# One PSUM pool for a whole decoder kernel, the norm's matmul inside the first up product, and wider operand operations

## The chip, the cores and the metric

The kernel runs on one core of a Trainium2 chip. The metric is the device time of one execution in microseconds (us); "before" is the kernel ahead of the change, "after" the changed one. Its engines are named as in the profile: PE (TensorE, matmuls), DVE (VectorE), ACT (ScalarE), POOL (GpSimd) and SP (SyncE, which here issues the weight loads). PSUM, the memory that PE writes to, has eight banks of 512 fp32 columns for each of the 128 partitions.

## The reference

A trunk of two pre-norm layers for one sequence of 512 tokens with 16 learned meta tokens ahead of them, model width 1024. Layer 0 mixes tokens by causal pooling, layer 1 by stick-breaking attention with 16 heads of 64; behind each mixer stands a SwiGLU FFN with 2816 hidden columns, and at the end a norm. Everything is float32.

```python
def rmsnorm(x, g):
    y = x * lax.rsqrt(jnp.mean(x * x, axis=-1, keepdims=True) + EPS)
    return y * g
def swiglu(h, w_gate, w_up, w_down):
    return (jax.nn.silu(h @ w_gate) * (h @ w_up)) @ w_down
# layer 0: window means (2, 4, 8, 16) minus the input, by group of 256 columns, times w, times scale
# layer 1: z = q k^T / 8; a = exp(log_sigmoid(z) + sum over later keys of log_sigmoid(-z)), strictly causal; a v, times w_o
for each layer:  x = x + mixer(rmsnorm(x)); x = x + swiglu(rmsnorm(x))
out = rmsnorm(x) without the meta tokens
```

## The kernel before, in words

**Numbers.** Every fp32 product is three matmuls on parts: a tile is cast to a shorter form on ACT ("hi", names ending in h) and the rest is subtracted on DVE ("lo", names ending in l); `mm3` (L106) issues hi·hi, hi·lo and lo·hi. Weights come by DMA into `wraw` (six buffers, SP's queue) and are split by `wsplit`: cast on ACT (L92), subtraction on DVE (L97).

**Stages.** The activations lie transposed as eight chunks h of 128 model columns by 528 tokens.

1. Start: norm of the tokens, pooling by matmuls with band matrices (`pool`), the group products (`mix`), and the residual add into h (L266). When a chunk is complete, `Norm.chunk` makes its hi and lo parts, times the gain (L152, L153), and adds its square to a running sum `acc` (L161; the last add is L128).
2. FFN of layer 0, 528 tokens. The hidden columns are worked in 22 steps f of 128. For f = 0, 1, 2 (`plain`) the gate and up products `pp` take the unnormalised hi and lo chunks; the norm's factor is multiplied in when a product is read out of PSUM (L364). The factor is one ones-matmul over `acc` (`norm_bcast`, L173, named fb0p), a reciprocal root on ACT (L135) and a Newton step on DVE (L136 to L139, result fb0r). From f = 3 on (`strassen`) gate and up are computed together as a 2 by 2 block product with seven instead of eight half products; their token operands are seven combinations of the normalised chunks. `operands` makes these once for each FFN: it multiplies in the norm (xn, L381), forms differences (t, L387) and splits into xh (ACT, L389) and xl (DVE, L390). The seven products run in three PSUM tiles pa, pb, pc; in between ACT copies the running values out (L412). The down product `pd` goes in six rounds; the down matmuls of one round are laid between the gate and up matmuls of the next. Its sums are added to h by DVE (L304).
3. Attention: eight head pairs p. Projections `pj`, scores z, sigmoids on ACT (L576), the running product over keys as a scan on DVE (L581), the weights sg (L583), their transposes on PE (`t`, L594 and L607), the product with v (`po`, L633). Output products `pw` come in three parts, for the pairs 0 to 1, 2 to 4 and 5 to 7; each is added to h by DVE (L660). The last part builds the next norm's chunks as it goes, with the names f1uh, f1ul, f1sq.
4. FFN of layer 1, on 512 tokens (fb1p and fb1r are its norm's factor), then the final norm and the store.

**What sets the order.** The program is written as one stream. A scheduler arranges each engine's instructions by its own estimate of times, bound by data dependences, by buffers coming free, and by `tc.issue_after(x)`, which keeps what is issued inside it behind instruction x. Each engine then works in that order, one after the other. An instruction that waits holds everything behind it on its engine. PSUM comes from four pools in turn, one for each stage (`phase`: ps0 with eight one-bank buffers, ps1 with six "w" and two "d", ps2 with four "one" and two "two" of two banks, ps3 like ps1). A new pool can be written only when the old one's tiles are read.

## Time and profile before

| what | value |
|---|---|
| runs | 1235.87, 1058.43, 1060.87 us; median 1060.87 |
| profiled execution | 1062.8 us, span 1061.0 us, mean granted PE clock 0.985 |
| busy in the span | PE 1023.1 (96%), DVE 856.6 (81%), ACT 556.9 (52%), POOL 6.2 (1%) |
| PE's longest waits | 4.1 (first product of FFN 1), 3.6 (last pair's transposes), 2.2 (first product of FFN 0), 2.1 (first Strassen products of FFN 0) |

Rows of the profile name the engine, the line of the kernel, the operation, the tiles as out<-in and their sizes, the count, and in brackets how long the engine was idle before it and what released it. In the table of stretches each engine's busy time stands with its number of instructions; a granted clock of 1.00 is full speed. A PE row's duration reaches past the start of the next row, since matmuls overlap; the distance of starts is what one costs. The stretches that matter: start until 39 us, FFN 0 to 408, attention to 691, FFN 1 to 1052, the store to 1061.

### The profile page before, as it was taken

Reading aid. Unit: us, or ns where it says so; the run is one execution under the profiler, and the core shown is the slowest. Engines: PE = TensorE matmul, PEld = TensorE weight load, DVE = VectorE, ACT = ScalarE, POOL = GpSimd, SP = SyncE. Lnnn points to the kernel's source line nnn. Section 1 sums busy time; section 2 is a strip of 40 time slices with the busy share of each in tenths; the row PEclk is TensorE's granted clock in tenths of the full one; section 3 lists DMA queues with packets and bytes.
Section 4 is the critical chain, followed back from the end, with each engine's and each line's share of the span. In section 5 each row is a group of like instructions: output and inputs, shape, how many; then the busy total and the mean of one; then the engine's idle time right before and its main releaser. Section 6 shows DMA issues by size and latency. Waiting matters only on the chain.

```text
span 1061.0 us, 18586 instructions
## 1 busy us (share of the span) xinstructions
PE 1023.1 (96%) x7302; PEld 949.3 (89%) x7302; DVE 856.6 (81%) x1529; ACT 556.9 (52%) x1131; POOL 6.2 (1%) x16
## 2 busy tenths in 40 slices
PE   8998999999999999999999998989999999999997
PEld 6997999999999998998888886867899999999985
DVE  7899987888878777678888987779977877788755
ACT  7555645454444455455555454555655444455544
POOL 1000000000000010000000000000000000000000
PEclk9999999999999999999999998989999999999999
DMA  9212323333333332211111211211223223333302
GB/s 351 72 51 69 128 94 100 101 100 100 100 100 100 99 120 82 78 40 61 40 51 37 69 58 66 80 62 58 100 100 115 84 100 99 100 100 120 109 31 80
DMA packets 43112, 95.73 MB, mean 90 GB/s; under 512 B 3328, under 2 KB 20096, under 8 KB 43024
## 3 DMA queue, kind: packets, MB, share of 16 engines
q1 hardware_dynamic: 42272, 93.40, 26.2%
q8 instruction: 57, 0.93, 0.3%
q10 hardware_dynamic: 752, 1.14, 0.3%
q14 instruction: 31, 0.25, 0.1%
HBM read 92.43 MB, written 2.10 MB: 89 GB/s over the span
## 4 chain that ended last, share of the span: by engine, by line
PE 78%; DVE 17%; issue 2%; ACT 1%; DMA 1%; SPq 0%; ACTq 0%; DVEq 0%
PE pb L106 15%; PE pd L106 11%; PE pd L331 11%; PE pa L106 10%; PE pc L106 10%; PE pj L106 9%; PE pp L106 4%; DVE kp L581 2%; PE pw L106 2%; PE z L567 2%; DVE xl L390 1%; DVE a L619 1%; PE t L594 1%; DVE t L387 1%; DVE sg L583 1%
## 5 line engine op out<-in xcount | busy, mean ns | idle before, releaser
L304 DVE TENSOR_TENSOR h<-pd,h 128x264 f32<-128x264 f32 x96 | 40.9, 427 | 14.0 <-PE pd L106 14.0
L92 ACT CAST ws_3h<-rgate 128x512 fp32r<-128x512 f32 x38 | 23.6, 620 | 53.3 <-PE pb L106 47.8
L581 DVE TENSOR_TENSOR_SCAN kp<-kp,estrip 128x1344 f32<-128x1344 f32 x16 | 47.3, 2954 | 3.8 <-ACT kp L576 3.4
L92 ACT CAST ws_4h<-s 128x512 fp32r<-128x512 f32 x38 | 23.6, 621 | 46.6 <-PE pa L106 27.7
L92 ACT CAST ws_5h<-s 128x512 fp32r<-128x512 f32 x38 | 23.6, 621 | 45.8 <-PE pb L106 34.7
L433 DVE TENSOR_TENSOR u<-pb,m 128x264 f32<-128x264 f32 (+1 forms) x38 | 16.3, 428 | 38.6 <-PE pb L106 38.6
L106 PE MATMUL pa<-xl,ws_0h 128*128 128x264 f32 (+1 forms) x152 | 43.3, 285 | 3.1 <-DVE xl L390 3.0
L106 PE MATMUL pb<-xl,ws_1h 128*128 128x264 f32 (+1 forms) x152 | 43.3, 285 | 1.0 <-DVE xl L390 1.0
L106 PE MATMUL pc<-xl,ws_2h 128*128 128x264 f32 (+1 forms) x152 | 43.1, 283 | 0.9 <-DVE xl L390 0.9
L106 PE MATMUL pb<-xh,ws_1h 128*128 128x264 f32 (+1 forms) x152 | 43.6, 287 | 0.2 <-ACT xh L389 0.2
L106 PE MATMUL pa<-xh,ws_3h 128*128 128x264 f32 (+1 forms) x152 | 43.6, 287 | 0.0
L106 PE MATMUL pa<-xl,ws_3h 128*128 128x264 f32 (+1 forms) x152 | 43.5, 286 | 0.0
L106 PE MATMUL pa<-xh,ws_3l 128*128 128x264 f32 (+1 forms) x152 | 43.3, 285 | 0.0
L106 PE MATMUL pc<-xh,ws_2l 128*128 128x264 f32 (+1 forms) x152 | 43.2, 284 | 0.0
L106 PE MATMUL pa<-xh,ws_0h 128*128 128x264 f32 (+1 forms) x152 | 43.1, 284 | 0.0
L106 PE MATMUL pb<-xh,ws_6l 128*128 128x264 f32 (+1 forms) x152 | 43.0, 283 | 0.0
L106 PE MATMUL pa<-xh,ws_0l 128*128 128x264 f32 (+1 forms) x152 | 43.0, 283 | 0.0
L106 PE MATMUL pb<-xh,ws_4l 128*128 128x264 f32 (+1 forms) x152 | 43.0, 283 | 0.0
L106 PE MATMUL pc<-xl,ws_5h 128*128 128x264 f32 (+1 forms) x152 | 42.9, 283 | 0.0
L106 PE MATMUL pb<-xh,ws_1l 128*128 128x264 f32 (+1 forms) x152 | 42.9, 283 | 0.0
L106 PE MATMUL pb<-xl,ws_4h 128*128 128x264 f32 (+1 forms) x152 | 42.9, 282 | 0.0
L106 PE MATMUL pc<-xh,ws_5h 128*128 128x264 f32 (+1 forms) x152 | 42.9, 282 | 0.0
(1179 smaller groups left out, 4110.9 us busy)
## 6 DMA issues: line engine op xcount, KB each, us to landing
rgate<-in_ffn_w_gate_dram SPq DMA_DIRECT2D x44, 512.0 KB, 3.5
rup<-in_ffn_w_up_dram SPq DMA_DIRECT2D x44, 512.0 KB, 3.5
rd<-in_ffn_w_down_dram SPq DMA_DIRECT2D x42, 512.0 KB, 3.6
rq<-in_sb_w_qkv_dram SPq DMA_DIRECT2D x8, 512.0 KB, 3.5
rk<-in_sb_w_qkv_dram SPq DMA_DIRECT2D x8, 512.0 KB, 3.4
rv<-in_sb_w_qkv_dram SPq DMA_DIRECT2D x8, 512.0 KB, 3.4
rwo<-in_sb_w_o_dram SPq DMA_DIRECT2D x8, 384.0 KB, 3.0
h<-in_x_t_dram SPq DMA_DIRECT2D x8, 264.0 KB, 6.9
```

The source lines that it names most:

```text
L92: nc.scalar.copy(hi, v[:, j:j + w])
L106: last = nc.tensor.matmul(o, lhsT=w, rhs=xx[:, sl], start=start and i == 0, stop=stop and i == 2, skip_group_check=more)
L304: nc.vector.tensor_tensor(out=hv, in0=pd, in1=hv, op=ALU.add)
L331: nc.tensor.matmul(pd, lhsT=hid[j][x_][:, ts], rhs=w_[:, sl], start=r > 0 and i + j == 0, stop=j == len(hid) - 1 and i == 2, skip_group_ch ...
L387: nc.vector.tensor_tensor(out=o, in0=a, in1=b, op=ALU.subtract)
L390: nc.vector.tensor_tensor(out=xl[i][:, m, :], in0=o, in1=f32(xh[i][:, m, :]), op=ALU.subtract)
L433: tt(out=u[:, a], in0=pb, in1=m1, op=ALU.add)
L567: nc.tensor.matmul(tz[:, hd, c:c + k1 - k0], lhsT=qq[hs, i * P:(i + 1) * P], rhs=kk[hs, k0:k1], start=j == 0 and c == 0, stop=False, skip_ ...
L581: nc.vector.tensor_tensor_scan(kp[:, hd, ::-1], kp[:, hd, ::-1], estrip[:, ::-1], 1.0, op0=ALU.mult, op1=ALU.max)
L583: return nc.vector.tensor_tensor(out=sg[:, hd, 0:STRIP - 1], in0=sg[:, hd, 0:STRIP - 1], in1=kp[:, hd, 1:STRIP], op=ALU.mult).ins
L594: nc.tensor.transpose(o, sg[:, c0:c0 + n], ident)
L619: nc.vector.scalar_tensor_tensor(a0[r, i], f32(a0h[r]), lo_rows[r], p2[r, 256:384], op0=ALU.mult, op1=ALU.add)
```

## The change

1. **One PSUM pool** for the whole program, with tags two (2 buffers of two banks), c and d (2 buffers of one bank each). At the start "any" takes turns over all of it; in the attention "one" takes turns over c and d. In `strassen` pa and pb become the two halves of one two-bank tile `pab`, pc takes c. A tile is tracked as a whole: an instruction that writes one half waits for reads of the other half too.
2. **The norm's matmul** stands inside the first up product, behind its fifth chunk (`FB = 4`), instead of behind the first gate product in the program's text. The weight splits of f = 1 are issued behind the last add of `acc` (`norm.done`), those of f = 2 behind the norm's factor. Gate and up are read out of PSUM after both products; SiLU works in place.
3. **Operands two chunks at a time**: the differences t are 8 instead of 16 DVE operations, xl 14 instead of 28, xh 14 instead of 28 ACT operations, each twice as wide.
4. **The attention's PE order is fixed**: `queued` issues each step behind the last instruction of the step before.

```diff
+    psum = ctx.enter_context(tc.tile_pool(name="psum", bufs=1, space=bass.MemoryType.PSUM))
+    turn = {"one": 0, "any": 0, "pair": 0}
     def ps(name, tag, banks=1):
+        i = turn.get(tag, 0)
+        turn[tag] = i + 1
+        if tag == "any":
+            if i % 8 in (0, 1, 4, 5):
+                if i % 2 == 0:
+                    turn["tile"] = ps(name, "two", 2)
+                return turn["tile"][:, i % 2]
+            tag = "cd"[i % 2]
+        if tag == "one":
+            tag = "cd"[i % 2]
         shape = [P, 512] if banks == 1 else [P, banks, 512]
-        return psum["pool"].tile(shape, F32, tag=tag, name=name, bufs=psum["bufs"][tag])
+        return psum.tile(shape, F32, tag=tag, name=name, bufs=2)
+    def ps_pair(name):
+        i = turn["pair"]
+        turn["pair"] = i + 1
+        if i % 3 == 2:
+            return [ps(f"{name}{j}", "c") for j in range(2)]
+        pt = ps(name, "two", 2)
+        return [pt[:, 0], pt[:, 1]]
...
             def plain(f):
-                parts = [wsplit(raw_gu(kind, f), f"w{kind}{f}") for kind in ("gate", "up")]
-                g, sg, u = (gw(f"{i}{f}") for i in ("g", "sg", "u"))
-                for dst, (wh, wl) in zip((g, u), parts):
-                    pts = [ps(f"pp{f}", "w")[:, :sl.stop - sl.start] for sl in pieces]
+                parts = []
+                for kind in ("gate", "up"):
+                    with tc.issue_after(norm.done if f == 1 else fst[1]) if f else nullcontext():
+                        parts.append(wsplit(raw_gu(kind, f), f"w{kind}{f}"))
+                g, u = (gw(f"{i}{f}") for i in "gu")
+                prods = []
+                both = ps_pair(f"pp{f}") if not full else None
+                for i, (dst, (wh, wl)) in enumerate(zip((g, u), parts)):
...
                     for k in range(KC):
-                        mm3([(t, slice(t0 + sl.start, t0 + sl.stop)) for t, sl in zip(pts, pieces)], wh[k], wl[k],
-                            uh[k], ul[k], k == 0, k == KC - 1)
-                    if not fst:
-                        fst.extend((norm_bcast([acc], f"fb{layer}", "d"), last_rstd[0]))
+                        with tc.issue_after(mark) if mark else nullcontext():
+                            last = mm3(...)
+                        if i == 1 and k == FB and not fst:
+                            with tc.issue_after(last):
+                                fst.extend((norm_bcast([acc], f"fb{layer}", "d"), last_rstd[0]))
+                            mark = last_bcast[0]
...
             def operands():
-                for m in range(4):
+                for m in (0, 2):
...
                     for i, o in enumerate((b11, t2, t1, b21, t3, b22, t4)):
-                        nc.scalar.copy(xh[i][:, m, :], o)
-                        nc.vector.tensor_tensor(out=xl[i][:, m, :], in0=o, in1=f32(xh[i][:, m, :]), op=ALU.subtract)
+                        hi, lo = xh[i][:, m:m + 2, :], xl[i][:, m:m + 2, :]
+                        nc.scalar.copy(hi, o)
+                        nc.vector.tensor_tensor(out=lo, in0=o, in1=f32(hi), op=ALU.subtract)
...
-                pa, pb, pc = [ps(f"p{i}{f}", "w")[:, :n] for i in "abc"]
+                pab = ps(f"pab{f}", "two", 2)
+                pa, pb, pc = pab[:, 0, :n], pab[:, 1, :n], ps(f"pc{f}", "c")[:, :n]
...
                 prod(pa, wa11, 0, True)
-                m1 = keep(pa, "m1")
+                nc.scalar.copy(m1, pa)
                 prod(pb, ws2, 1, True)
...
+        pos = []
+        def queue():
+            return tc.issue_after(pos[0]) if pos else nullcontext()
+        def queued(*steps):
+            for st in steps:
+                with queue():
+                    pos[:] = [st()]
...
-            mark = None
-            for st in before:
-                mark = st()
-            with tc.issue_after(mark) if mark else nullcontext():
-                sc.group(0)
-                mark = sc.group(1)
-            for st in between:
-                with tc.issue_after(mark):
-                    mark = st()
-            with tc.issue_after(mark):
-                sc.group(2)
+            queued(*before, lambda: (sc.group(0), sc.group(1))[1], *between, lambda: sc.group(2))
```

How instructions move is shown at three places. On DVE at the start of the second FFN, before: f1sq is the norm's running sum, fb1t the Newton step, wgate2l the low part of f = 2's gate weights. This is the end of the sum.

```order
L161 TENSOR_TENSOR f1sq_8384<-f1sq_8384,f1sq_8521 128x528
L128 SCALAR_TENSOR_TENSOR f1sq_8384<-f1sq_8543,f1sq_8384 128x528
L97 TENSOR_TENSOR wgate2l_8849<-rgate_2_8846,wgate2h_8848 128x512
L97 TENSOR_TENSOR wgate2l_8853<-rgate_2_8846,wgate2h_8852 128x512
L136 TENSOR_TENSOR fb1t<-fb1r 128x528
L97 TENSOR_TENSOR wup2l_8859<-rup_2_8856,wup2h_8858 128x512
```

The same place on DVE in the changed kernel, where wgate1l and wup1l are f = 1's weights:

```order
L147 SCALAR_TENSOR_TENSOR f1sq_8237<-f1sq_8396,f1sq_8237 128x528
L116 TENSOR_TENSOR wgate1l_8567<-rgate_1_8564,wgate1h_8566 128x512
L116 TENSOR_TENSOR wgate1l_8571<-rgate_1_8564,wgate1h_8570 128x512
L116 TENSOR_TENSOR wup1l_8577<-rup_1_8574,wup1h_8576 128x512
L116 TENSOR_TENSOR wup1l_8581<-rup_1_8574,wup1h_8580 128x512
L155 TENSOR_TENSOR fb1t<-fb1r 128x528
L157 SCALAR_TENSOR_TENSOR fb1t<-fb1p_8479,fb1t 128x264
```

f = 1's subtractions have moved from among the sum's adds to behind it, and f = 2's from ahead of the Newton step to behind it. At the start of the first FFN the same four stand behind the sum. On PE the norm's matmul (fb0p, fb1p) stands behind 82 and 43 matmuls of the products, before behind 89 and 33.

On PE at the last head pair, before: z_416 is the last score group, pw_2 and pw_3 are output products of the pairs 2 to 4.

```order
L106 MATMUL pw_2_8163<-os4h,wo_2l_8160 128x512
L106 MATMUL pw_3_8178<-os2h,wo_3h_8174 128x512
L106 MATMUL pw_3_8178<-os2l,wo_3h_8174 128x512
L106 MATMUL pw_3_8178<-os2h,wo_3l_8175 128x512
L567 MATMUL z_416_8136<-qk_1h,qk_0h 128x400 [waits PE_49,Activation_49]
```

The same place on PE in the changed kernel:

```order
L125 MATMUL pw_1_7978<-os4l,wo_1h_7974 128x512
L125 MATMUL pw_1_7978<-os4h,wo_1l_7975 128x512
L598 MATMUL z_416_7989<-qk_1h,qk_0h 128x400 x2
L598 MATMUL z_416_7989<-qk_1h,qk_0h 128x16 x2
L598 MATMUL z_416_7989<-qk_1l,qk_0h 128x400 x2
```

The scores now follow pw_1 directly; the nine matmuls of pw_2 and the first three of pw_3 stand behind them.

On PE in a Strassen step of the first FFN, in the changed kernel: pc is the third product, pd_0 a down product, pab with ws_1h the first matmul of pb.

```order
L125 MATMUL pc_2507<-xl_547,ws_2h_2486 128x264
L125 MATMUL pc_2507<-xh_540,ws_2l_2487 128x264
L125 MATMUL pd_0_2618<-hh_1760,wd_2_0h_2614 128x264 [waits DVE_49,Activation_49]
L125 MATMUL pd_0_2618<-hl_1761,wd_2_0h_2614 128x264
L125 MATMUL pd_0_2632<-hh_1760,wd_2_0h_2614 128x264 [waits DVE_49]
L125 MATMUL pd_0_2632<-hl_1761,wd_2_0h_2614 128x264
L125 MATMUL pab_2506<-xh_539,ws_1h_2482 128x264 [waits Activation_49]
```

Before, pb's first matmul stands there without a wait, and behind other matmuls:

```order
L106 MATMUL pd_7_2547<-hh_1651,wd_1_7h_2529 128x264
L106 MATMUL pd_7_2547<-hl_1652,wd_1_7h_2529 128x264
L106 MATMUL pd_7_2547<-hh_1651,wd_1_7l_2530 128x264
L106 MATMUL pb_2602<-xh_551,ws_1h_2577 128x264
L106 MATMUL pb_2602<-xl_558,ws_1h_2577 128x264
```

Now that matmul waits for ACT's copy of the other half, which reads pa's product; between pa's last matmul and the wait stand typically sixteen matmuls.

More of the change, by code (lines that the diff above doesn't have):

```diff
@@ L126, in add_eps @@
     def add_eps(out, sq, acc):
-        nc.vector.scalar_tensor_tensor(out, sq, D * EPS / P, acc, op0=ALU.add, op1=ALU.add)
-    last_rstd = []
+        return nc.vector.scalar_tensor_tensor(out, sq, D * EPS / P, acc, op0=ALU.add, op1=ALU.add).ins
+    last_rstd, last_bcast = [], []
     def rstd_of(parts, r, t):
@@ L172, in norm_bcast @@
             for i, acc in enumerate(accs):
-                nc.tensor.matmul(p, lhsT=ones, rhs=acc[:, o:o + h], start=i == 0, stop=i == len(accs) - 1)
+                last_bcast[:] = [nc.tensor.matmul(p, lhsT=ones, rhs=acc[:, o:o + h], start=i == 0,
+                                                  stop=i == len(accs) - 1).ins]
             parts.append((p, slice(o, o + h)))
@@ L179, in trunk @@
     norm = Norm(16, "f0")
-    with tc.tile_pool(name="start", bufs=1) as sp, phase("ps0", one=8):
+    with tc.tile_pool(name="start", bufs=1) as sp:
         nc.scalar.activation(sp.tile([P, 1], F32, name="table"), ones[:, 0:1], AF.Abs_reciprocal_sqrt)
@@ L232, in trunk @@
         nc.vector.memset(warm, 0.0)
-        pw = ps("warm", "one")
+        pw = ps("warm", "any")
         for _ in range(WARM):
@@ L244, in trunk @@
                 cs = slice(c * P, (c + 1) * P)
-                pp = ps(f"pool{c}{hf}", "one")[:, :HALF]
+                pp = ps(f"pool{c}{hf}", "any")[:, :HALF]
                 for j, (i, off) in enumerate(terms):
@@ L259, in trunk @@
                 g, d = c // 2, c % 2
-                pm = ps(f"mix{c}{hf}", "one")[:, :HALF]
+                pm = ps(f"mix{c}{hf}", "any")[:, :HALF]
                 for k in range(2):
@@ L375, in operands @@
                 rb = fst[0]
[L376 removed]
+                for m in (0, 2):
                     xn = []
                     for c in (m, m + 4):
[L379 to L382 removed]
+                        t = fp.tile([P, 2, L], F32, tag="xn", name=f"xn{c}", bufs=2)
+                        for j in range(2):
+                            gc = gains[:, gcol + c + j:gcol + c + j + 1]
+                            nc.vector.scalar_tensor_tensor(t[:, j, tok], hT[c + j][:, tok], gc, rb[:, tok],
+                                                           op0=ALU.mult, op1=ALU.mult)
                         xn.append(t)
[L384 removed]
+                    b11, b12, b21, b22 = [t[:, :, s] for t in xn for s in halves]
                     t1, t2, t3, t4 = [wk(f"t{i}") for i in range(4)]
@@ L480, in before_attention @@
         return norms[0].chunk
-    with phase("ps1", w=6, d=2):
-        ffn(0, 16, norm, before_attention)
-    with tc.tile_pool(name="att", bufs=1) as ap, phase("ps2", one=4, two=2):
+    ffn(0, 16, norm, before_attention)
+    with tc.tile_pool(name="att", bufs=1) as ap:
         uh, ul, acc = norms[0].uh, norms[0].ul, norms[0].acc
@@ L599, in turned @@
             p1, p2 = ps(f"t1{p}{hd}", "two", 2), ps(f"t2{p}{hd}", "one")
-            for i in range(4):
-                tr(p1[:, 0, i * P:(i + 1) * P], i, 1)
-            for i in range(1, 4):
-                tr(p1[:, 1, (i - 1) * P:i * P], i, 2)
-            tr(p1[:, 1, 384:512], 3, 4)
-            for i in range(2, 4):
-                tr(p2[:, (i - 2) * P:(i - 1) * P], i, 3)
-            nc.tensor.transpose(p2[:, 256:384], am.rearrange("p a b -> p (a b)"), ident)
+            with queue():
+                for i in range(4):
+                    tr(p1[:, 0, i * P:(i + 1) * P], i, 1)
+                for i in range(1, 4):
+                    tr(p1[:, 1, (i - 1) * P:i * P], i, 2)
+                tr(p1[:, 1, 384:512], 3, 4)
+                for i in range(2, 4):
+                    tr(p2[:, (i - 2) * P:(i - 1) * P], i, 3)
+                pos[:] = [nc.tensor.transpose(p2[:, 256:384], am.rearrange("p a b -> p (a b)"), ident).ins]
             a1 = [ap.tile([P, 2, 512], F32R, tag="a1", name=f"a1{p}{hd}{n}", bufs=2) for n in "hl"]
@@ L686, in trunk @@
         sg = begin(0, got, [], steps[3:4])
-        steps[4]()
+        queued(steps[4])
         values()
         nxt, steps, values = proj(1)
-        for st in steps[:3]:
-            st()
+        queued(*steps[:3])
         early, w = wo(0, 2), wo(2, 5)
@@ L696, in trunk @@
             w0 = turned(p, 0, sg[:, 0])
-            for st in steps[3:] if p + 1 < NP else w[4:6]:
-                st()
+            queued(*(steps[3:] if p + 1 < NP else w[4:6]))
             if p + 1 < NP:
                 values()
-            attend(p, 0, w0, v, of)
+            queued(lambda: attend(p, 0, w0, v, of))
             w1 = turned(p, 1, sg[:, 1])
```

56 lines of the change are left out of this document (24 added, 32 removed).

## The prediction, on record before the changed kernel ran

> **What bounds the kernel now.** I read the page first, then the busy time by stretches of the run, then what TensorE (PE) waited for, and last single instructions at the places where it waited. All times are microseconds of one profiled execution, whose span is 1061.0 and whose own time is 1062.8; the median of the three runs shown, 1060.87, lies 1.9 below it. The page gives busy time, share and instruction count of each engine, and the engines' shares of the chain of waits:
>
> ```profile
> PE 1023.1 (96%) x7302; PEld 949.3 (89%) x7302; DVE 856.6 (81%) x1529; ACT 556.9 (52%) x1131; POOL 6.2 (1%) x16
> PE 78%; DVE 17%; issue 2%; ACT 1%; DMA 1%; SPq 0%; ACTq 0%; DVEq 0%
> ```
>
> PE is idle for 1061.0 − 1023.1 = 38 in all, and the change leaves every matmul product as it is. Only this idle time and the time lost at a lower clock can be won. The stretches tell where both lie (start:end and width, then busy time and instructions of PE, PEld, DVE, ACT, POOL, the granted PE clock, DMA share, GB/s):
>
> ```profile
> 26.00:40.00 14.00, 11.81 (x93) 11.63 (x93) 12.84 (x28) 7.68 (x14) 0.00 (x0) 0.96 0.26 90
> 40.00:60.00 20.00, 20.00 (x155) 19.87 (x154) 16.92 (x31) 10.92 (x20) 0.00 (x0) 0.94 0.21 70
> 80.00:90.00 10.00, 6.39 (x34) 5.51 (x33) 10.00 (x24) 4.30 (x13) 0.00 (x0) 0.83 0.15 52
> ...
> 250.00:381.00 131.00, 131.00 (x1078) 131.00 (x1077) 100.99 (x189) 64.06 (x129) 0.00 (x0) 1.00 0.32 105
> ...
> 410.00:440.00 30.00, 28.38 (x185) 24.79 (x184) 17.72 (x22) 15.04 (x26) 0.00 (x0) 0.94 0.15 53
> ...
> 500.00:670.00 170.00, 160.91 (x1096) 140.21 (x1096) 142.90 (x201) 89.73 (x192) 0.00 (x0) 0.98 0.16 51
> ...
> 690.00:710.00 20.00, 15.85 (x58) 12.47 (x57) 14.03 (x23) 9.21 (x16) 0.00 (x0) 0.83 0.23 79
> 710.00:740.00 30.00, 28.95 (x139) 23.65 (x137) 29.97 (x61) 16.65 (x35) 0.00 (x0) 1.00 0.15 53
> 740.00:760.00 20.00, 18.47 (x123) 17.03 (x124) 18.99 (x42) 13.44 (x32) 0.00 (x0) 0.91 0.23 79
> ...
> 800.00:1030.00 230.00, 230.00 (x1603) 214.41 (x1602) 179.21 (x318) 116.66 (x238) 0.00 (x0) 1.00 0.30 99
> 1030.00:1061.00 31.00, 23.06 (x120) 19.43 (x118) 16.76 (x47) 12.48 (x31) 0.00 (x0) 0.92 0.18 68
> ```
>
> In the steady parts of both FFNs (250:381, 800:1030) PE is never idle and the clock is 1.00: there is nothing to win there, only to lose. The borders are otherwise: around the start of the first FFN (26 to 90), the end of attention and the start of the second FFN (690 to 760), where DVE is full (10.00 of 10, 29.97 of 30) and PE waits for it. What PE waited for (total, times, longest):
>
> ```profile
> PE pp L106 <- DVE h L660: 4.1, 1, 4.1
> PE t L594 <- DVE sg L583: 3.6, 1, 3.6
> PE pa L106 <- DVE xl L390: 3.0, 3, 2.1
> PE pp L106 <- DVE h L266: 2.2, 1, 2.2
> ```
>
> Four places: the first product of each FFN, the last head pair of attention, and the Strassen products waiting for their low operands xl. In all of them DVE is the releaser.
>
> **The change part by part. Start of the first FFN.** From the last mix matmuls to the operands:
>
> ```profile
> 36.59 0.28 PE L106 MATMUL mix<-ph,pw1l 128*128 128x264 f32 x1
> 39.06 0.56 PE L106 MATMUL pp<-f0uh,wgate0h 128*128 128x264 f32 x1 [2.19 <-DVE h L266]
> 47.92 0.71 DVE L128 SCALAR_TENSOR_TENSOR f0sq<-f0sq,f0sq 128x528 f32<-128x528 f32 x1
> 51.42 1.05 PE L173 MATMUL fb0p<-f0sq,ones 128*128 128x264 f32 x4
> 52.93 0.71 DVE L136 TENSOR_TENSOR fb0t<-fb0r 128x528 f32<-128x528 f32 x1 [2.16 <-ACT fb0r L135]
> 97.20 1.11 DVE L390 TENSOR_TENSOR xl<-t,xh 128x264 fp32r<-128x264 f32 x3
> ```
>
> The first product waited for the last read out of the old PSUM pool. With one pool it starts behind the mixes, so the 2.19 goes. Half of it may come back ahead of it: pool and mix products that are halves of one two-bank tile wait until both halves of its last use are read. Neither decides: what is late next is the norm. Its sum is complete at 47.92 + 0.71 = 48.6, but its matmul stood behind the whole product and ran at 51.42. Now it stands inside the up product; it can run at about 48.9. The four subtractions of f=1's weights now stand between the sum and L155 (L136 before) on DVE, in order, and hold it until 48.6 + 4 × 0.6 = about 51.1 instead of 52.93, with 0.6 as one of them takes in the next rows: 1.8 gained. These are DVE's starts for a wide operation and two half as wide:
>
> ```profile
> 60.44 0.70 DVE L367 TENSOR_TENSOR u<-sg,u 128x528 f32<-128x528 f32 x1
> 61.06 0.42 DVE L387 TENSOR_TENSOR t<-xn 128x264 f32<-128x264 f32 x1
> 61.40 0.76 DVE L364 TENSOR_TENSOR g<-pp,fb0r 128x264 f32<-128x264 f32 x2
> ```
>
> From start to start, 0.62 for 528 columns and 0.34 for 264. So one wide operation for two saves 2 × 0.34 − 0.62 = 0.06, and the 8 + 14 fewer operations of the operands save 22 × 0.06 = 1.3 in each FFN. ACT's 14 fewer casts are worth nothing, since DVE, not ACT, is full here. [...]
>
> Between L155 and the last xl, DVE worked 97.20 + 1.11 − 52.93 = 45.4. By the new order it has 1.3 less for the wider operations, three weight subtractions more (3 × 0.6) and four evictions of down products fewer (4 × 0.34): 44.5. The last xl is then ready at 51.1 + 44.5 = 95.6, some 2.7 earlier. But those evictions are missing because some 40 down matmuls now lie behind the last wait instead of before it, at 0.12 each almost 5 of PE time, about half of which PE can do while the last operands arrive. I take +0.5 for this border: from −1.5 (all 40 left over) to +4 (PE finds them all in the time that it now idles).
>
> **First FFN to attention.** The first projection is now laid between the last down products. PE is idle there for 30 − 28.38 = 1.6, and the norm that the attention needs comes when it came: 0, from −1 to +1.
>
> **Attention.** The fixed order of pairs 0 to 4 is that of the scheduler before, on PE, DVE and ACT. In pairs 5 and 6 the transposes go behind all four output products instead of two. Of the 170 − 160.91 = 9.1 idle in that stretch, 3.6 is the last pair's; the rest is spread over all pairs: +0.5, from 0 to 1.5. The last pair:
>
> ```profile
> 648.84 0.40 PE L106 MATMUL pw<-os2h,wo_3h 128*128 128x512 f32 x1
> 649.07 0.39 PE L106 MATMUL pw<-os2l,wo_3h 128*128 128x512 f32 x1
> ...
> 649.63 0.46 PE L567 MATMUL z<-qk_1h,qk_0h 64*128 64x400 f32 x4
> 651.83 2.96 DVE L581 TENSOR_TENSOR_SCAN kp<-kp,estrip 128x1344 f32<-128x1344 f32 x1 [1.64 <-ACT kp L576]
> 655.76 1.55 DVE L583 TENSOR_TENSOR sg<-sg,kp 128x1343 f32<-128x1343 f32 x1
> 657.45 2.36 PE L594 MATMUL t<-consts,sg 128*128 128x128 f32 x10 [3.59 <-DVE sg L583]
> ```
>
> The last scores z stood behind twelve matmuls of pw_2 and pw_3; now they stand ahead of them: 12 × 0.23 = 2.8 earlier. The scan, the weights and the transposes follow, so the 3.59 shrinks to about 0.8: +2.8, and everything after it moves up alike, since it hangs on sg. Bounds: 0, if the output evictions on DVE (0.7 each) slip ahead of the scan and eat it; +4.5, if the clock loss behind the gap (PEclk 0.98 of 170, so 3.4) half goes too.
>
> **Attention to the second FFN.**
>
> ```profile
> 690.62 0.40 PE L106 MATMUL pw<-os7h,wo_7l 128*128 128x512 f32 x1
> 695.16 0.77 PE L106 MATMUL pp<-f1uh,wgate0h 128*128 128x512 f32 x1 [4.15 <-DVE h L660]
> 700.49 0.71 DVE L128 SCALAR_TENSOR_TENSOR f1sq<-f1sq,f1sq 128x528 f32<-128x528 f32 x1
> 705.60 0.61 PE L173 MATMUL fb1p<-f1sq,ones 128*128 128x264 f32 x2
> 708.29 0.71 DVE L136 TENSOR_TENSOR fb1t<-fb1r 128x528 f32<-128x528 f32 x1 [2.30 <-ACT fb1r L135]
> 748.38 0.75 DVE L390 TENSOR_TENSOR xl<-t,xh 128x256 fp32r<-128x256 f32 x2
> ```
>
> Here the product now starts at 690.9 and runs at 0.23 a matmul; before, it ran at half clock for 6.8 (0.17 of the clock missing over 20 is 3.4 lost). 43 matmuls then stand ahead of the norm's: 690.9 + 42 × 0.23 = 700.5, against 705.60. The sum must be there by then: it ended at 701.2, and the four subtractions that moved behind it (4 × 0.6 = 2.4) bring it to 698.8. L155 follows at the old distance (2.7), at 703.2 against 708.29: 5.1. DVE's work from there to the last xl, 749.1 − 708.29 = 40.8, loses 1.3 and gains two subtractions of f=2's weights that stood before L136: −0.1. PE reaches the same count of matmuls at about 744.8 instead of 749.9: +5. Lower bound +2, if the product's own chunks arrive late (PE takes them as fast as DVE makes them, and half the gain goes); upper +7, if the half clock at 740:760 (0.91 of 20, so 1.8 lost) goes as well.
>
> **Steady parts.** With pa and pb as halves of one tile, pb's first product waits for ACT's copy of pa. Both PE and all behind it would stand:
>
> ```profile
> L412 ACT COPY m<-pa x38: 354/372/383, 94.7 to 1020.0; 128x264 f32<-128x264 f32 x19, 128x256 f32<-128x256 f32 x19
> ```
>
> The copy takes 0.37; between the end of pa's product and that wait stand, by the new order, typically 12 pc and 4 down matmuls, 16 × 0.12 = 1.9, which cover it: 0. ACT is busy for 64.06 of 131, so it is seldom far behind. The SiLU written in place and the scratch tiles regrouped by two change no operation's size: 0. The weight loads on SP's queue wait for raw buffers that the moved subtractions free 2.4 later; DMA is busy for 0.23 of 690:710, and the loads run ahead by several tiles: 0. The tail (31 − 23.06 idle) keeps its work: 0.
>
> **Sum**: 0.5 + 0 + 0.5 + 2.8 + 5 = 8.8, so 1062.8 − 8.8 = 1054.0; against the median, 1052.1. I take 1053.
>
> **The rivals.** *All the gaps go.* The waits of the four places (4.1 + 3.6 + 3.0 + 2.2 = 12.9) and the clock lost at 26:60, 80:90, 500:670 and 690:760 (0.6 + 1.2 + 1.7 + 3.4 + 3.4 + 1.8 = 12.1): 25, hence 1038, more than 2% faster. For it: each has DVE as its releaser, and DVE is given less to do. Against: DVE stays full through both operand stages, and so PE must wait somewhere. The clock fell after the 2.19 gap at 39.06 (0.56 for a matmul instead of 0.28). [...] Chance 0.12.
>
> *No gain.* DVE stays the bound through both operand stages, and what the norm gains is lost to the work moved behind it: only the last pair's 2.8 is left and the first border loses 1.5: about 1061. For it: the first border's working above. Chance 0.25.
>
> *Slower: the shared tile.* At three places of each of the 38 Strassen steps (pb's first matmul, pa's second product, pb's third) PE waits for ACT's copy. If ACT stands behind its own casts there, each shows up. Uncovered, 114 × 0.37 = 42, so 1054 + 42 = 1096; beyond 2% it needs 1082 − 1054 = 28, which is 0.25 a wait. Against: the 1.9 of cover and ACT's 52%. For: the steady rows have no slack at all. Chance 0.07.
>
> *The change doesn't do what it says*: fixing the attention's order fixes what stood there already. That is in the sum, which counts only pairs 5 to 7.
>
> **How the numbers follow.** Forecast 0.56, no gain 0.25, all gaps go 0.12, shared tile 0.07. A measurement of this kernel tells about 2% (21) from no change: faster means under 1040, slower over 1082. The forecast's own range from its bounds is 1062.8 − 18 to 1062.8 + 0.5, so 1045 to 1063. The no-gain rival lies inside it. Reaching half-way towards the rival on the fast side, and by 2 over the upper bound for the scatter of the three runs (1058.43 against 1060.87), 1041 to 1065 should hold 8 in 10. Faster 0.12, within 2% 0.81, slower 0.07.
>
> **What would show it.** Right: pp directly behind mix and pw; fb1p about 5 earlier from the last pw; the wait of t on sg below 1.5; the rows 250:381 and 800:1030 still full. Wrong: waits of pab on ACT m in the steady part; DVE's span from L155 to the last xl not shorter than 44 and 40; a new wait of PE on DVE behind the last xl, or a half clock behind a gap that stayed.

## The result, and the profile after

The changed kernel took 1066.59 us in the median of four runs (1066.33 to 1066.9), the kernel before 1060.77 over the runs taken by then, one of which took 1235.87; without that one the ratio is 1.0062 with a 95% interval of 1.0043 to 1.0082. It is slower by 0.6%, about 6 us, where 8 to 9 us of gain were forecast, and outside the range. The two profiled executions lie closer together, with spans of 1064.8 and 1061.0.

The page of the changed kernel gives for the engines and for the chain of waits:

```profile
PE 1023.8 (96%) x7302; PEld 948.7 (89%) x7302; DVE 857.5 (81%) x1485; ACT 549.9 (52%) x1103; POOL 7.2 (1%) x16
PE 79%; DVE 16%; ACT 2%; issue 2%; DMA 1%; SPq 0%; ACTq 0%; DVEq 0%
```

DVE has 44 instructions fewer, exactly the 2 × 22 of the operands, and is busy for as long as before; PE too. The stretches of the changed kernel (columns as in the prediction):

```profile
12.00:26.00 14.00, 10.65 (x66) 10.23 (x66) 12.31 (x23) 10.97 (x22) 0.00 (x0) 0.76 1.04 394
26.00:40.00 14.00, 14.00 (x115) 13.87 (x114) 9.88 (x21) 3.61 (x8) 0.00 (x0) 1.00 0.16 57
40.00:60.00 20.00, 19.35 (x148) 18.29 (x147) 18.37 (x31) 14.02 (x26) 0.00 (x0) 1.00 0.16 49
...
80.00:90.00 10.00, 5.09 (x23) 4.07 (x22) 10.00 (x19) 4.37 (x8) 0.00 (x0) 0.66 0.01 4
90.00:100.00 10.00, 8.97 (x62) 8.67 (x63) 10.00 (x21) 5.32 (x11) 0.00 (x0) 0.83 0.24 80
...
250.00:381.00 131.00, 131.00 (x1077) 131.00 (x1077) 101.57 (x191) 61.81 (x130) 0.00 (x0) 1.00 0.31 101
...
690.00:710.00 20.00, 20.00 (x88) 16.19 (x87) 17.46 (x28) 14.18 (x25) 0.00 (x0) 1.00 0.32 105
710.00:740.00 30.00, 26.01 (x121) 20.77 (x119) 29.97 (x50) 14.52 (x24) 0.00 (x0) 0.98 0.22 71
740.00:760.00 20.00, 17.86 (x112) 16.57 (x113) 17.48 (x31) 12.33 (x26) 0.00 (x0) 0.78 0.16 54
...
800.00:1030.00 230.00, 230.00 (x1590) 213.69 (x1589) 183.59 (x323) 115.55 (x236) 0.00 (x0) 1.00 0.31 99
```

And two of the kernel before that the prediction did not show:

```profile
12.00:26.00 14.00, 12.37 (x98) 11.67 (x97) 13.17 (x26) 12.78 (x28) 0.00 (x0) 1.00 1.04 394
90.00:100.00 10.00, 9.16 (x63) 8.06 (x63) 10.00 (x25) 6.22 (x17) 0.00 (x0) 1.00 0.09 28
```

The pool changes are gone as forecast: 26:40 and 690:710 are full at full clock. The steady parts are as full as before. What was won at these two places came back elsewhere: at the start (12:26, PE 10.65 instead of 12.37, clock 0.76 instead of 1.00) and in both operand stages (80:90 at a clock of 0.66 instead of 0.83; 740:760 at 0.78 instead of 0.91). What PE waited for now:

```profile
PE pab L125 <- DVE xl L424: 5.0, 2, 2.5
PE pool L268 <- DVE pl L275: 3.4, 2, 2.7
PE pd L351 <- ACT hh L369: 2.6, 1, 2.6
PE pd L351 <- DVE hl L370: 2.6, 1, 2.6
...
PE t L636 <- DVE sg L614: 0.8, 1, 0.8
```

The wait of t on sg fell from 3.6 to 0.8, as forecast. The three longest new waits are pool on pl, pd on hh and pd on hl.

To see where the time goes, I counted PE's matmuls in each trace from the start, each weighted by its columns, and asked how much later (+) or earlier (−) than the kernel before a kernel has issued the same amount. The first column is the kernel before's own time; "end" is the difference of the spans. Each column compares two single executions, so it shows where a kernel wins or loses, while the medians tell how much: the trace of before lies 2 us over its median (its granted clock is 0.985, against 0.987 or 0.988 in most other runs of it), those of e7, e11 and e12 2.1, 2.3 and 3.2 over theirs. The experiments' columns belong to the next section.

| place (us of before) | after | e7 four pools | e8 four pools, one chunk | e9 order alone | e10 norm alone | e11 wide alone | e12 mixed pools |
|---|---|---|---|---|---|---|---|
| 50, first product of FFN 0 | +2.0 | −1.1 | −1.3 | +0.2 | −1.3 | +0.3 | −2.4 |
| 100, operands of FFN 0 made | +3.7 | +1.1 | −0.8 | +0.6 | −0.7 | +0.5 | −1.7 |
| 380, end of the steady part | +3.8 | +1.0 | −0.7 | +0.6 | −0.7 | +0.6 | −1.7 |
| 450, in the attention | +6.4 | +1.4 | −2.2 | +0.5 | −2.2 | +0.5 | −3.0 |
| 640, ahead of the last pair | +6.6 | +1.7 | −1.9 | +0.8 | −2.2 | +0.4 | −2.7 |
| 690, end of the attention | +5.0 | −1.6 | −5.3 | −2.5 | −2.4 | +0.3 | −4.4 |
| 720, products of FFN 1 | −2.2 | −4.6 | −8.2 | −2.8 | −5.3 | +0.3 | −11.5 |
| 780, operands of FFN 1 made | +2.6 | −2.9 | −7.9 | −6.2 | −5.0 | +1.9 | −10.0 |
| 1000 | +2.4 | −2.9 | −7.9 | −6.1 | −5.0 | +1.9 | −10.0 |
| end | +3.8 | −2.9 | −7.9 | −6.1 | −4.9 | +1.9 | −7.0 |

So the changed kernel loses 3.7 up to 100, 2.6 between 380 and 450, and 1.4 behind 1000; it wins 1.6 at the last pair and 7.2 at the second FFN's start, of which the operand stage there takes 4.8 back. The rows at these places follow. The start of the changed kernel:

```profile
19.89 0.59 PE L268 MATMUL pool<-band,ah 128*128 128x264 f32 x1 [2.71 <-DVE pl L275]
...
51.91 0.70 DVE L147 SCALAR_TENSOR_TENSOR f0sq<-f0sq,f0sq 128x528 f32<-128x528 f32 x1
...
52.66 1.16 PE L192 MATMUL fb0p<-f0sq,ones 128*128 128x264 f32 x4
...
54.93 0.70 DVE L155 TENSOR_TENSOR fb0t<-fb0r 128x528 f32<-128x528 f32 x1
...
96.22 1.33 DVE L424 TENSOR_TENSOR xl<-t,xh 128x528 fp32r<-128x528 f32 x2
```

The norm's sum ends at 52.6 instead of 48.6, and the Newton step comes at 54.93, 2.0 later than before instead of 1.8 earlier. The first FFN's end, in the changed kernel and then in the kernel before (the last add of the attention's norm, and that norm's matmul):

```profile
419.96 0.70 DVE L147 SCALAR_TENSOR_TENSOR ansq<-ansq,ansq 128x528 f32<-128x528 f32 x1
...
420.72 1.16 PE L192 MATMUL abp<-ansq,ones 128*128 128x264 f32 x4
```

```profile
411.18 0.70 DVE L128 SCALAR_TENSOR_TENSOR ansq<-ansq,ansq 128x528 f32<-128x528 f32 x1
...
414.47 1.05 PE L173 MATMUL abp<-ansq,ones 128*128 128x264 f32 x4
```

The norm's matmul comes 6.25 later, of which 3.8 was lost before. The last pair of the changed kernel:

```profile
655.67 2.96 DVE L612 TENSOR_TENSOR_SCAN kp<-kp,estrip 128x1344 f32<-128x1344 f32 x1 [0.94 <-ACT kp L607]
...
659.60 1.55 DVE L614 TENSOR_TENSOR sg<-sg,kp 128x1343 f32<-128x1343 f32 x1
...
661.30 1.28 PE L636 MATMUL t<-consts,sg 128*128 128x128 f32 x10 [0.83 <-DVE sg L614]
...
668.56 0.50 PE L676 MATMUL po<-a170l,vv 128*128 128x512 f32 x1 [1.31 <-DVE a170l L659]
```

Against its place in the run (+6.6) the transposes come 2.8 earlier (657.45 + 6.6 − 661.30), the forecast's figure. The second FFN's start and the tail:

```profile
695.82 0.39 PE L125 MATMUL pw<-os7h,wo_7l 128*128 128x512 f32 x1
...
705.79 1.05 PE L192 MATMUL fb1p<-f1sq,ones 128*128 128x264 f32 x4
708.48 0.71 DVE L155 TENSOR_TENSOR fb1t<-fb1r 128x528 f32<-128x528 f32 x1 [2.23 <-ACT fb1r L154]
...
737.63 0.50 PE L351 MATMUL pd<-wd_0h,hl 128*128 128x512 f32 x1 [2.58 <-DVE hl L370]
741.37 0.58 PE L125 MATMUL pab<-xl,ws_0h 128*128 128x256 f32 x1 [2.48 <-DVE xl L424]
747.25 1.89 DVE L424 TENSOR_TENSOR xl<-t,xh 128x512 fp32r<-128x512 f32 x3
...
1044.17 0.50 PE L351 MATMUL pd<-wd_0h,hh 128*128 128x512 f32 x1 [2.62 <-ACT hh L369]
```

### The profile page after: what moved, and what is told of

It is laid out like the page before. It is cut to its first block, busy times and chain, and to the rows that moved or that the text cites. A ratio compares the mean times of both kernels' runs of the same rounds, so it can differ in the third digit from the quotient of the medians.

```text
span 1064.8 us, 18519 instructions
## 1 busy us (share of the span) xinstructions
PE 1023.8 (96%) x7302; PEld 948.7 (89%) x7302; DVE 857.5 (81%) x1485; ACT 549.9 (52%) x1103; POOL 7.2 (1%) x16
## 4 chain that ended last, share of the span: by engine, by line
PE 79%; DVE 16%; ACT 2%; issue 2%; DMA 1%; SPq 0%; ACTq 0%; DVEq 0%
PE pab L125 26%; PE pd L125 11%; PE pd L351 11%; PE pc L125 10%; PE pj L125 9%; PE pw L125 3%; PE pp L125 2%; DVE kp L612 2%; PE z L598 2%; DVE a L662 1%; DVE xl L424 1%; DVE sg L614 1%; PE t L636 1%; PE mix L125 1%; DVE xn L414 1%
## 5 line engine op out<-in xcount | busy, mean ns | idle before, releaser
L125 PE MATMUL pab<-xl,ws_0h 128*128 128x264 f32 (+1 forms) x152 | 43.8, 288 | 5.0 <-DVE xl L424 5.0
L324 DVE TENSOR_TENSOR h<-pd,h 128x264 f32<-128x264 f32 x96 | 40.7, 427 | 7.4 <-PE pd L125 7.2
L125 PE MATMUL pab<-xh,ws_0h 128*128 128x264 f32 (+1 forms) x152 | 43.4, 285 | 1.1 <-ACT xh L423 1.1
L125 PE MATMUL pc<-xh,ws_2h 128*128 128x264 f32 (+1 forms) x152 | 43.3, 285 | 1.1 <-DVE u L396 1.1
L125 PE MATMUL pab<-xh,ws_0l 128*128 128x264 f32 (+1 forms) x152 | 43.7, 287 | 0.0
L125 PE MATMUL pab<-xh,ws_6l 128*128 128x264 f32 (+1 forms) x152 | 43.0, 283 | 0.0
L125 PE MATMUL pab<-xh,ws_4l 128*128 128x264 f32 (+1 forms) x152 | 43.0, 283 | 0.0
L125 PE MATMUL pab<-xh,ws_1h 128*128 128x264 f32 (+1 forms) x152 | 43.0, 283 | 0.0
L125 PE MATMUL pab<-xl,ws_1h 128*128 128x264 f32 (+1 forms) x152 | 43.0, 283 | 0.0
L125 PE MATMUL pab<-xl,ws_3h 128*128 128x264 f32 (+1 forms) x152 | 43.0, 283 | 0.0
L125 PE MATMUL pab<-xl,ws_6h 128*128 128x264 f32 (+1 forms) x152 | 42.9, 282 | 0.0
```

The source lines that it names most:

```text
L125: last = nc.tensor.matmul(o, lhsT=w, rhs=xx[:, sl], start=start and i == 0, stop=stop and i == 2, skip_group_check=more)
L324: nc.vector.tensor_tensor(out=hv, in0=pd, in1=hv, op=ALU.add)
```

## The experiments

The theory after this result (A): the places of loss are separate, and the one pool makes most of them. Rivals: the wide operands make the loss (B), or the splits and read-outs moved by the new plain step do (C). Every edit also lets the scheduler arrange anew, so I read each experiment by its columns of the table up to the place of its edit, and the time as a whole with that in mind. First, parts of the change undone one at a time.

**e1, the start's banks.**

```diff
-    turn = {"one": 0, "any": 0, "pair": 0}
+    turn = {"one": 0, "any": 2, "pair": 0}
```

> The changed kernel with one number different: the start's turn over the banks begins at a one-bank tile, so the warm-up product no longer shares a two-bank tile with the first pool product, and the pool products reuse a bank after eight products again instead of seven. Theory A (the start lost about 2 us by its pool products waiting for reads of the other half, and the half clock behind that wait): the 2.7 us wait of pool on pl and the half clock at 18 to 25 us go, the norm's matmul comes at about 51 instead of 52.7, and the time is 1064 to 1065 instead of 1066.6. Rival (the start is hidden, because DVE sets when the operands are ready): the waits go, the time stays within 0.5 of 1066.6.

Measured: 1068.99 us, ratio to before 1.0076 (1.006 to 1.0093). The wait of pool on pl went from the list, but the half clock stayed (18.8 to 25.6). PE stood at +0.8 at 50 us instead of +2.0, and at +3.1 at 380 instead of +3.8. Then, 340 us behind the edit, the new order holds a new wait of a down matmul on hh (2.0) and a stretch at half clock (394.2 to 397.7), which cost 3.8 (from +3.1 at 380 to +6.9 at 410, where the changed kernel stayed at +3.8). Both expectations on the time are refuted: the start wins about 1 as such, and a single number at the start moves the scheduler's choices far away by more than that.

**e2, operands one chunk at a time.** The loops of `operands` as before the change, on halves of the wide scratch tiles:

```diff
-                for m in (0, 2):
+                for m in range(4):
...
-                        nc.scalar.copy(hi, o)
+                        nc.scalar.copy(xh[i][:, m, :], o)
```

> The changed kernel with the operands made one chunk at a time, as before the change. Theory A (the wide operations save DVE time, and the loss is elsewhere): DVE's span from the Newton step to the last xl grows by 1.3 us in each FFN, and the time is 1067 to 1069. Rival B (wide operations make the first Strassen products wait longer for a complete set, which brings the 10 us at half clock in both FFNs): PE's waits for xl of 2.5 us go, the half clock shrinks to some 3.4 us in each, and the time is 1060 to 1063.

Measured: 1062.87 us, 1.0028 (1.0017 to 1.0039), 3.7 faster than the changed kernel. DVE's span from the Newton step to the last xl grew as A said and more (47.9 instead of 43.8 in the first FFN, 45.2 instead of 40.7 in the second). Of the second's 4.5 the operands' own share is 1.5, by the starts of its rows (28 xl and 16 t at 0.34 instead of 14 and 8 at 0.60); the rest is five other operations that now stand ahead of the last xl. And yet PE lost less in the second operand stage: from −3.5 at 720 to −1.9 at 780, instead of from −2.2 to +2.6. The half clock there fell from 10.2 us (738.6 to 748.8) to 3.4 (738.0 to 741.5), and the waits of 2.5 for xl went in both FFNs. B holds for the second FFN. In the first, the wide operands were 0.7 better at 100 us (+3.7 against +4.4): there PE now waited 5.4 for down products to be read (pd on h).

**e3, the plain step as before** (norm's matmul behind the gate product in the text, splits not held back, each product read out behind itself):

```diff
-                        if i == 1 and k == FB and not fst:
-                            with tc.issue_after(last):
-                                fst.extend((norm_bcast([acc], f"fb{layer}", "d"), last_rstd[0]))
+                    if not fst:
+                        fst.extend((norm_bcast([acc], f"fb{layer}", "d"), last_rstd[0]))
```

> The changed kernel with the plain products, the norm's matmul, the weight splits of the steps 1 and 2 and the read-outs issued as before the change. Theory A (the earlier norm is the part that gains, 5 us at the second FFN's start): the Newton step of the second FFN comes 3 to 5 us later from the last output product, and the time is 1068 to 1072. Rival C (the splits held back and the read-outs only after both products pile DVE work up in the operand stage, where PE then waits 2.6 us for hl and falls to half clock): the wait of pd for hl goes and the time is 1061 to 1064.

Measured: 1072.6 us, 1.0112 (1.0097 to 1.0127). The Newton step came at 59.5 and 715.3 instead of 54.9 and 708.5. From the last output product to the Newton step of the second FFN it took 6.6 longer, more than A's 3 to 5. The wait of pd on hl did go, as C said, but two others came in its place, both for halves of two-bank tiles:

```profile
PE pab L125 <- DVE u L386: 4.2, 1, 4.2
PE pab L125 <- ACT ma L438: 3.5, 1, 3.5
```

So A's direction holds and C's time does not. By the count of matmuls the old step had cost 2.5 at 1000 (+4.9 instead of +2.4). The rest of the 6 came at the tail, where a stretch at half clock (1046.0 to 1052.9) took 3.1 that the changed kernel did not lose; why it fell there is not shown.

**e4, the attention order left free**, with the score groups held in order as before the change.

```diff
         def queue():
-            return tc.issue_after(pos[0]) if pos else nullcontext()
+            return nullcontext()
```

> The changed kernel with the attention's PE order left to the scheduler again. Theory A (the fixed order gains at the last pair by putting the scores ahead, and gives half of it back because the second head's transposes stand behind an attend product that waits): 1066.5 to 1068.5. Rival (the free order interleaves transposes and attend products at the last pair and gains): 1063.5 to 1065.5, with the idle time of PE in the last pair below 3 us.

Measured: 1075.69 us, 1.0138 (1.0123 to 1.0154); 9 slower, where A gave 2 at most. PE's waits of t on sg rose from 0.8 to 9.9, over five of them. With the one pool the scheduler does not find again the order that it found with four pools: the fixed order does not only fix what stood there, it holds up what the pool would have spoilt.

**e5, more banks for the tail**, and **e6, the projections behind the downs.** In e5 the last down products of the second column half alternate between a one-bank tile and half of a two-bank tile (tag x in the diff):

```diff
-                    down_n(r, t, e, prev, ws[e], "dc"[e], sl)
+                    down_n(r, t, e, prev, ws[e], "x" if e else "d", sl)
```

```diff
         for st in steps[:3]:
-            st()
+            with tc.issue_after(last_down[0]):
+                st()
```

> The changed kernel, with the last down products of the second column half (e = 1) taking turns over a one-bank tile and half of a two-bank tile, so four instead of two of them can be open, as six were before the change. Theory A (with two, PE has no down matmuls left to cover the last hidden split, and waits 2.6 us for hh near the end): that wait goes and the time is 1063.5 to 1065.2 instead of 1066.6. Rival (the last split is the end of the chain either way; the time it takes is only moved): the time stays within 0.7 of 1066.6.

Measured: 1065.88 us, 1.0054 (1.0033 to 1.0076), 0.7 under the changed kernel. PE's wait near the end went from 2.6 (for hh) to 1.0 (for u), and its last matmul came at 1055.12 instead of 1058.07; but the span ended only 1.2 earlier, and 1.0 of that was there at 50 us already. The rival holds, at the edge of its 0.7. The traces show where the gain went: from the last add into hn to ACT's last scaling (the last two steps before the store) it took 2.07 in the changed kernel, but 3.48 in e5 and 3.47 in the kernel before. Where PE ends earlier, the last squares and the scaling of the token tile before still pass through ACT one after another (1055.93 to 1058.06 in e5) ahead of that last scaling.

> The changed kernel, with the attention's first three projection steps held behind the first FFN's last down matmul, as they stood before the change. Theory A (with one pool the scheduler lays the projections between the last down products; that delays the norm, for which PE then waits; it cost 2.6 us at the first border): the norm's matmul comes about 2.5 us earlier and PE's count of matmuls behind it is 2 to 3 us ahead of the changed kernel at 450 us; the time is 1063.5 to 1065. Rival (the projections have to be done either way, so the order does not matter): within 0.7 of 1066.6.

Measured: 1061.91 us, 1.0025 (1.0015 to 1.0036), 4.7 faster. The norm's matmul in e6:

```profile
418.75 1.05 PE L192 MATMUL abp<-ansq,ones 128*128 128x264 f32 x4
```

2.0 earlier than in the changed kernel, though PE was 0.5 further behind ahead of it (+4.3 against +3.8 at 380). Behind it PE stands at +3.0 at 450 instead of +6.4, of which 1.7 is a half-clock stretch (431.4 to 434.8) that did not come. Between 640 and 690 it wins 3.3 where the changed kernel won 1.6, again a half-clock stretch less. So two half-clock stretches fewer, 3.4 in all, are a good part of the 4.7. A holds beside them: without the 1.7 of clock e6 still wins 2.2 between 380 and 450, most of the 2.6 that the changed kernel lost there. With one pool, projection matmuls become possible among the last downs, the scheduler takes them, and they delay the downs on whose sums the norm waits.

**e7, four pools again**, all else of the change kept, and **e8, four pools and one chunk.**

```diff
-    with tc.tile_pool(name="start", bufs=1) as sp:
+    with tc.tile_pool(name="start", bufs=1) as sp, phase("ps0", one=8):
...
-                pab = ps(f"pab{f}", "two", 2)
-                pa, pb, pc = pab[:, 0, :n], pab[:, 1, :n], ps(f"pc{f}", "c")[:, :n]
+                pa, pb, pc = [ps(f"p{i}{f}", "w")[:, :n] for i in "abc"]
...
-    ffn(0, 16, norm, before_attention)
+    with phase("ps1", w=6, d=2):
+        ffn(0, 16, norm, before_attention)
```

> The changed kernel with four PSUM pools again, as before the change; the norm's place, the wide operands and the fixed order stay. Theory A (the one pool makes most of the loss: about 2 at the start, 2.6 at the first FFN's end, 1.4 to 2.6 at the tail, against 2.4 won at pool changes): 1061 to 1064. Rival B (the wide operands and the half clock behind them make it): 1065 to 1068.

Measured: 1057.78 us, 0.9979 (0.9965 to 0.9992); its runs scatter from 1054.5 to 1059.9. The median is 8.8 under the changed kernel, more than A gave. The start in e7:

```profile
18.35 0.39 PE L260 MATMUL pool<-band,al 128*128 128x264 f32 x1 [0.93 <-DVE al L237]
19.54 0.43 PE L260 MATMUL pool<-band,al 128*128 128x264 f32 x1 [0.69 <-DVE al L237]
...
51.02 0.71 DVE L146 TENSOR_TENSOR fb0t<-fb0r 128x528 f32<-128x528 f32 x1 [0.64 <-ACT fb0r L145]
```

The Newton step comes at 51.0, where the prediction had put it (51.1): its working of the norm was right for four pools. In the table, e7 lies 3.1 ahead of the changed kernel at 50, 5.0 at 450, 6.6 at 690, and 6.7 at the end. Its longest wait is that of the operand stages, once in each FFN:

```profile
PE pa L116 <- DVE xl L414: 7.0, 2, 3.6
```

> Four pools and operands one chunk at a time, so only the norm's place with the plain step's new order, and the fixed attention order, are left of the change. Theory A and B together (both the pool and the wide operands lose, the norm's place wins 4 to 5 at the second FFN): 1055 to 1059, faster than the kernel before. Rival (the norm's place does not win as the operand stage stays DVE's): 1060 to 1063.

Measured: 1054.97 us, 0.9953 (0.9938 to 0.9968): faster than the kernel before by 4 to 6 us, and 2.8 faster than e7. The longest wait on xl is now:

```profile
PE pb L116 <- DVE xl L412: 1.2, 1, 1.2
```

The wide operands lose with four pools too, and what they lose is mostly clock: the two runs of e7 with a granted clock as high as e8's (0.990 and 0.992) took 1054.84 and 1054.53, no longer than e8.

Then each of the three other parts alone, on the kernel before's four pools (SiLU in place in all of them), and a mixture.

**e9, the attention order alone** (e8 with the plain step as in e3).

> Of the change only the fixed attention order is kept (with SiLU in place): four pools, the plain step and the norm as before, operands one chunk at a time. Theory A (the scores ahead of pw_2 and pw_3 at the last pair win the forecast 2.8 to 3.5): PE's count of matmuls at 690 us is 3 to 4 us further than in the kernel before, relative to 640 us; the time is 1055.5 to 1057.5. Rival (it fixes what stood there): 1059.5 to 1061.

Measured: 1057.06 us, 0.9967 (0.9956 to 0.9979). At the last pair:

```profile
655.46 1.28 PE L613 MATMUL t<-consts,sg 128*128 128x128 f32 x10 [0.83 <-DVE sg L591]
```

From 640 to 690 it wins 3.3 (from +0.8 to −2.5), the size that A gave. But its way there is another. The transposes' wait shrank by 2.8, and new waits took most of it back, above all one that the kernel before does not have:

```profile
PE po L653 <- DVE a170l L636: 1.3, 1, 1.3
```

Over the same matmuls PE stood idle for 3.1 instead of 4.2. The larger part, 3.0, is the half clock of the kernel before (656.7 to 663.5), which e9 does not have. A further 3.4 in the table, between 720 and 780, is no part of A; the median, 3.1 under the kernel before, does not show a gain of 6.

**e10, the plain step alone** (e8 with the order free as in e4).

> Of the change only the plain step is kept: the norm's matmul inside the up product, splits held back, read-outs after both products; four pools, operands one chunk at a time, the attention order free. Theory A (it wins 2 to 3 at the second FFN and about 1 at the first): 1056 to 1058. Rival (what wins is the attention order, the plain step nothing): 1059 to 1061.

Measured: 1057.88 us, 0.9971 (0.9958 to 0.9984). It wins 0.7 up to 100, and 2.6 from 690 to 780. The half-clock stretch at 425, which is missing here and in e8, gives 1.5 more at 450. A holds.

**e11, the wide operands alone** (e7 with the plain step as in e3 and the order free).

> Of the change only the wide operands are kept (with SiLU in place): four pools, the plain step as before, the attention order free. Theory B (wide operands shorten DVE's stage but make PE wait longer for a complete set, with more time at half clock): 1062 to 1065, with 2 to 5 us more at half clock than before in the two operand stages. Rival, the step of the prediction (22 operations fewer, 1.3 us in each FFN): 1057.5 to 1059.

Measured: 1062.33 us, 1.0026 (1.0013 to 1.0039): slower, as B says and against the prediction's step. Two stretches of e11:

```profile
80.00:90.00 10.00, 6.17 (x27) 5.16 (x26) 10.00 (x20) 4.69 (x10) 0.00 (x0) 0.68 0.17 53
90.00:100.00 10.00, 10.00 (x69) 9.99 (x69) 9.34 (x20) 5.27 (x12) 0.00 (x0) 0.81 0.22 68
```

DVE finished the first FFN's operands at 95.1 instead of 98.3, and PE idled a little less over the two stretches (10 − 6.17 = 3.8, against 3.6 + 0.8 = 4.4 before). But the clock was low for longer: (0.32 + 0.19) × 10 = 5.1 lost, against 1.7 before: 17.1 us at half clock in the two operand stages instead of 6.8, a larger rise than B's 2 to 5. The 3.4 more lost to it here eat the 3.2 that DVE won. In the second FFN the wait itself grew too; PE waited 1.9 for xh ahead of pb and 1.4 for hl, and 1.6 was lost (+0.3 to +1.9). Whether a filled gap would have kept the gain was not tried.

**e12, a mixture:** own pools for the start and the first FFN, one pool for the attention and the second FFN, operands one chunk at a time.

```diff
+    ctx.enter_context(phase("ps2", two=2, c=2, d=2))
-    with tc.tile_pool(name="att", bufs=1) as ap, phase("ps2", one=4, two=2):
+    with tc.tile_pool(name="att", bufs=1) as ap:
-    ctx.enter_context(phase("ps3", w=6, d=2))
```

> Own pools for the start and for the first FFN, one pool for attention and the second FFN; operands one chunk at a time; the norm's place and the fixed order stay. Theory A (the one pool wins about 3 at the second FFN's start, where no pool change holds up the first product, and loses 1.4 at the tail and more at the first FFN): 1052 to 1054. Rival (the operand stage of the second FFN, which DVE sets, takes the 3 back): 1055 to 1057.

Measured: 1052.59 us, 0.9925 (0.9908 to 0.9942), the fastest of all, 7.5 under the kernel before. From 690 to 780 it wins 5.6, against 2.6 with four pools (e8) and 2.4 in the changed kernel. A holds. At the tail 3.0 is lost, of which 1.7 is a half-clock stretch (1032.9 to 1036.3) behind the wait for hh that comes first here; then 45 us of e12 from its Newton step on, and the same of the changed kernel:

```profile
1031.78 0.50 PE L353 MATMUL pd<-wd_0h,hh 128*128 128x512 f32 x1 [2.62 <-ACT hh L371]
```

The operand stage of e12:

```profile
699.00:744.00 45.00, 40.79 (x211) 34.06 (x210) 44.80 (x94) 26.36 (x58) 0.00 (x0) 0.96 0.21 69
```

The same in the changed kernel:

```profile
708.40:753.40 45.00, 38.87 (x185) 32.03 (x184) 44.07 (x73) 24.21 (x43) 0.00 (x0) 0.89 0.20 69
```

PE idled 4.2 in e12 and 6.1 in the changed kernel, and the clock was 0.96 against 0.89, though DVE is full in both.

## Why the prediction was wrong, point by point

The span moved by +3.8 where −8.8 was forecast, a difference of 12.6. Its terms, by the table:

- **Start of the first FFN: +0.5 won forecast, 3.7 lost.** Two steps failed. "Half of it may come back ahead of it" undersized what the one pool does at the start: the norm's sum came 4.0 later, and e7 has the Newton step at the forecast time, so it is the pool. Without the new wait of 2.7 on pl (e1) the sum comes 1.3 earlier at the same half clock (6.8); e5 and e6, with that wait but a half clock of 3.4, gain about 1.0. What makes up the rest is not shown. The second step is the operand stage, 1.7 more lost. A late norm isn't its cause: e7, with the norm in time, loses 2.2 between 50 and 100, and e8, with one chunk at a time, 0.5.
- **First FFN to attention: 0 forecast, 2.6 lost.** The prediction saw that the projections stand among the last downs, and said that the norm "comes when it came". It did not ask what the downs pay for it. e6 shows the price, about 2.2.
- **Attention: +3.3 won forecast, 1.6 measured, 3.3 in e9.** The gap at t closed as forecast, from 3.6 to 0.8. The step that failed is "everything after it moves up alike": PE then waits at po, and its idle time over these matmuls fell by 1.1, not 2.8. That e9 still wins 3.3 is partly luck, for 3.0 of it is a half clock that went, which the prediction had in its upper bound alone. In the changed kernel a half-clock stretch (670.3 to 673.7) takes 1.7 of that back; e2, with the same order on PE there, has none and wins 3.4.
- **Second FFN: +5 won forecast, 2.4 kept.** The working of the norm held: 4.8 gained at L155 (708.29 + 5.0 − 708.48). DVE's stage took 40.65 against the forecast 40.7. What failed is that PE would follow DVE: PE stood for 2.6 at pd for hl and 2.5 at pab for xl, and ran at half clock for 10.2. With operands one chunk at a time the forecast size comes out: 5.5 in e2, 5.6 in e12.
- **The wide operands: 1.3 won in each FFN by the starts of the rows.** DVE's side was right: 1.5 by the rows of e2 (e11's first stage, from the Newton step at 53.2 to the last xl at 95.1, was 3.5 shorter, where the order changed as well). Its worth for PE was wrong in sign: e11 1.0026, and e8 against e7 2.8. The prediction named the sign of this failure ("a half clock behind a gap that stayed"), but gave it no price.
- **Steady parts and shared tile: 0, right.** 131.00 of 131 and 230.00 of 230; no wait on ACT's copies shows. The rival that would have made the kernel 2% slower did not come; a long wait of that kind stands in e3 alone, 3.5 once.
- **Tail: 0 forecast, 1.4 lost**, 3.0 in e12. The step that failed is "keeps its work", which left out the banks: the second column half has two instead of six there, PE waits 2.6 for the last hidden split, and its last matmul comes 2.9 later against its place at 1000. The span loses half of that, since ACT's last steps are done sooner behind PE's end; e5 gave PE 1.5 of it back and the span nothing.
- **The rivals.** "No gain" (1061) named the right cause, that DVE's stage takes back what the norm wins, but no case priced losses at the start, at the border and at the tail together. "Fixes what stood there already" missed a case: the fixed order is worth 9 us with one pool (e4).

## What to carry to other kernels

Sharing one buffer pool across stages does not only remove the wait at the stage change: it lengthens how long a buffer is held where its parts are tracked as one (PE waited 2.7 on pl at the start here), and it lets a scheduler move work early that something else is waiting behind (2.2 at the first FFN's end, by e6). Price both before counting the wait as won. When a fast engine waits for a slower one that is always full, saving the slower one time helps only if the results that release the fast one come sooner one by one; fewer, wider operations released it later here (longest wait on xl 3.6 in e7, 1.2 in e8), and with the idle time packed into one longer gap the clock was lower besides (0.985 to 0.988 in eight of e7's ten runs, 0.989 and 0.990 in e8's). And an edit that a scheduler sees can move more at a far place than it wins at its own (e1).
